# Seven quarter products in place of eight for two token blocks of the up-projections, with the blocks' order turned round

## The chip, the cores and the metric

One Trainium2 chip, one of its cores. The metric is the device time of one execution in microseconds (us); the median of several executions is compared.

## The reference, cut to what matters

One decoder layer over 1072 token columns: 32 sample tokens, 16 meta tokens and 1024 prompt tokens, model width 1024. Retention and gated DeltaNet heads are mixed first; the change lies behind them, in the output projection and the gated MLP:

```python
x = x + jnp.concatenate([o_ret, o_gdn], axis=-1) @ w_out          # 1024 x 1024
u, buf = causal_depthwise_conv(rms_norm(x, norm_ffn) @ w_up, ...) # 1024 x 5632, width 3
gate, val = jnp.split(u, 2, axis=-1)                              # 2816 each
x = x + (jax.nn.silu(gate) * val) @ w_down                        # 2816 x 1024
y = rms_norm(x, norm_final)
```

The meta tokens are dropped at the end, so the MLP works on 1058 columns (32 sample columns, 2 meta columns that the convolution needs, 1024). Outputs are float32.

## The kernel before

**Precision.** Each operand of the large projections is kept as two float32r tensors, a rounded high part and the rest: `split` casts on ScalarE and subtracts on VectorE or GpSimd. A product is three matmuls per 128 rows of the contraction: high x high, high x low, low x high (`mm3`). Tokens lie along the free dimension, features on the partitions.

**How the order is set.** Every operation is recorded with its inputs and outputs (`Recorder.add`, all instructions have line 466) and placed by a list scheduler in `flush`: per engine, the ready operation with the lowest class goes first, then the one recorded first; the costs are written into `_cost`. Buffers come from rings (`ring`, `buf`): a tile gets a slot when the planner places its first operation, in the order in which tiles were first used within their stream. The resulting order of each engine is fixed in the program. Loads are issued by SyncE (SP).

**Stages.** Up to about 630 us: input projections and head mixing. Then the part in `cp`: the last gate, and the output projection by three token blocks `BLK_B` of 384, 384 and 290 columns: `out_split` makes high and low parts of the mixed heads, `out_tile` makes one 128-row tile of one block (24 matmuls), adds the residual on VectorE, squares on ScalarE and adds the square up. Blocks 0 and 1 run together over the eight tiles of `w_out`, then block 2 with the same weights loaded again, while `norm_steps` of blocks 0 and 1 runs: sum of squares through PE, a root on VectorE (`rsqrt`), the root spread over partitions through PE, and eight normed and split tiles into `hh` and `hl`. The first gate and value tile of `w_up` are projected for blocks 0 and 1 (`early`) before block 2's norm.

**The pair loop.** For each of 22 pairs of a gate tile and a value tile: `up` loads the 1024 x 128 weights in two halves of 512 columns through `raw` into `whi`, `wlo` (two buffers each), does 24 matmuls for each of the three blocks (384, 386 and 292 columns, two of overlap for the convolution) into a bank of ring `mm` (three banks), and applies the width-3 convolution out of PSUM: one ScalarE instruction and two on VectorE. Sample columns have their own convolution with the state `su`, loaded whole at the start. Then Silu on ScalarE, gate times value on GpSimd, and a split of the result. After every second pair, `down` adds 8 tiles x 3 blocks to the residual `ob`: six matmuls into a bank of ring `mx` (five banks) and one VectorE addition each; `w_down` comes in pieces of 512 columns, split by ScalarE and GpSimd. Matmuls of projections have class 2, down sums class 1, weight splits and what empties PSUM class 0. The last two pairs end in `final`: down sums block by block, the closing norm, and the stores.

Of the kernel before, what the change touches and what calls it, by code (L numbers as in the profile page):

```python
# [45 lines left out]
BLK_B = ((0, 384), (384, 768), (768, 1058))  # L46
# [433 lines left out]
def build(tc, I, O, debug=None):  # L480
# [33 lines left out]
    ring(const, "whi", 2, KD * P, F32R)  # L514
    ring(const, "wlo", 2, KD * P, F32R)
# [48 lines left out]
    def load_w(src, lo_eng=None, tags=("raw", "raw")):  # L564
        with cls(0):
            hi = buf("whi", [P, KD, P])
            lo = buf("wlo", [P, KD, P])
            for a, tag in zip((0, 4), tags):
                raw = buf(tag, [P, 4, P])
                dma(out=raw, in_=src[:, a:a + 4, :])  # L570
                split(hi[:, a:a + 4, :], lo[:, a:a + 4, :], raw, lo_eng or V)
        return hi, lo
# [35 lines left out]
    def gate_proj(slot, nxt, tag):  # L608
# [7 lines left out]
        proj(gate_tile(slot), nxt, evac)  # L616

    with tc.tile_pool(name="mp", bufs=1) as mp:
# [78 lines left out]
        g1 = buf("whi", [P, KD, P])  # L697
        g2 = buf("wlo", [P, KD, P])
# [527 lines left out]
        keep = [v.vt for t in wq.values() for v in t]  # L1226
# [8 lines left out]
    with tc.tile_pool(name="cp", bufs=1) as cp:  # L1235
        for tag, n, e, dt in (("r15", 20, 384, F32R), ("dhl", 8, 512, F32R), ("f2k", 12, 512, F32), ("us", 1, 512, F32), ("wr", 2, 512, F32),
                              ("uo", 2, 72, F32), ("c3", 6, 4, F32)):
            ring(cp, tag, n, e, dt)
        su = cp.tile([P, 2 * NF, NB, 6], F32, name="su")
        dma(out=su, in_=I["sff"].rearrange("p (f b t) -> p f b t", f=2 * NF, b=NB))  # L1240

        def f384():
            return buf("f2k", [P, 384])

        gate_proj(3, None, "f2k")

        KS = (0, 4, 1, 5, 2, 6, 7, 3)
        wtags = (("wr", "wr"), ("raw", "raw"))
# [3 lines left out]
        def pieces(t):  # L1252
            c0, c1 = BLK_B[t]
            return ((0, NS, 0), (NS, c1, NS + 14)) if t == 0 else ((0, c1 - c0, c0 + 14),)

        def out_split(t):
            c0, c1 = BLK_B[t]
            n = c1 - c0
            if t == 0:
                o_in[t] = [[buf("r15", [P, 384]) for _ in range(KD)] for _ in range(2)]  # L1260
# [3 lines left out]
            for k in KS:  # L1264
                for a, b, s0 in pieces(t):
                    split(oh[k][:, a:b], ol[k][:, a:b], ob[:, k, s0:s0 + b - a], V if k % 2 else G)
# [5 lines left out]
            acc_of[t] = f384()  # L1272

        def out_weights(i):
            while len(wo) < min(2 * KD, i + 3):
                q = len(wo)
                wo.append(load_w(w_out[q % KD], None, wtags[q % 2]))

        def out_tile(w, m, t):
            c0, c1 = BLK_B[t]  # L1280
# [8 lines left out]
            if m == 0:  # L1289
                S.activation(acc[:, 0:n], y, AF.Square)  # L1290
            else:
                sq = f384()
                S.activation(sq[:, 0:n], y, AF.Square)
                V.tensor_tensor(out=acc[:, 0:n], in0=acc[:, 0:n], in1=sq[:, 0:n], op=ALU.add)

        def norm_block(t, acc, level=1):
            with cls(level):
                yield from norm_steps(t, acc)

        def norm_steps(t, acc):  # L1300
            c0, c1 = BLK_B[t]
            n = c1 - c0
            yield

            pss = bank()
            col, ct_, cm = (buf("c3", [P, 3]) for _ in range(3))
# [3 lines left out]
            for i, (a, b) in enumerate(cuts):  # L1310
                if b - a < P:
                    G.memset(cm, 1.0)
            ssc = buf("c3", [P, 3])
            if n % P:
                G.memset(ssc, 1.0)
                nf_ = n // P
                V.tensor_copy(ssc[:, 0:nf_], pss[:, 0:nf_])
                V.tensor_copy(ssc[0:n % P, nf_:nf_ + 1], pss[0:n % P, nf_:nf_ + 1])
            else:
                V.tensor_copy(ssc, pss[:, 0:3])  # L1320
            rsqrt(col, ssc, ct_, cm, 1.0 / D)
            yield
            rb = bank()
            dg = buf("us", [P, 3, P])
# [3 lines left out]
            for m in range(KD):  # L1328
                if m % 2 == 0:
                    yield  # L1330
                h2 = f384()
                V.scalar_tensor_tensor(out=h2[:, 0:n], in0=ob[:, m, c0:c1], scalar=nffn(m), in1=rb[:, 0:n], op0=ALU.mult, op1=ALU.mult)
                split(hh[:, m, c0:c1], hl[:, m, c0:c1], h2[:, 0:n], V if m % 2 else G)

        out_split(0)
        out_split(1)
        out_weights(0)
        for m, t in ((0, 0), (1, 0), (0, 1), (1, 1)):
            out_tile(m, m, t)
        for m in range(2, KD):  # L1340
            out_weights(m)
            for t in (0, 1):
                out_tile(m, m, t)
        out_split(2)
        others = [norm_block(0, acc_of[0]), norm_block(1, acc_of[1])]
        for m in range(KD):
            out_weights(KD + m)
            out_tile(KD + m, m, 2)
            for _ in range(5):
                next(others[m // 2 % 2], None)  # L1350
        for o in others:
            for _ in o:
                pass

        UP = ((0, 384), (382, 768), (766, 1058))

        def up(f, uo, dsts, ts=(0, 1, 2), part=None):
            hi, lo = part or load_w(w_up[f])
            i = 2 * (f // NF) + f % 2
            for t in ts:  # L1360
                b0, b1 = UP[t]
                nh = b1 - b0
                out = bank("mm")
                mm3(out[:, 0:nh], hi, lo, lambda k: hh[:, k, b0:b1], lambda k: hl[:, k, b0:b1])
                d = f384()
                dsts.append(d)
                o0, s = (NS - 2, NS) if t == 0 else (0, 0)
                n = nh - 2 - o0
                with cls(0):
                    S.activation(d[:, s:s + n], out[:, o0:o0 + n], AF.Copy, scale=cf(0, f))  # L1370
                    V.scalar_tensor_tensor(out=d[:, s:s + n], in0=out[:, o0 + 1:o0 + 1 + n], scalar=cf(1, f), in1=d[:, s:s + n],
                                           op0=ALU.mult, op1=ALU.add)
                    V.scalar_tensor_tensor(out=d[:, s:s + n], in0=out[:, o0 + 2:o0 + 2 + n], scalar=cf(2, f), in1=d[:, s:s + n],
                                           op0=ALU.mult, op1=ALU.add)
                    if t == 0:
                        S.copy(su[:, f, :, 2:6], out[:, 0:NS].rearrange("p (b t) -> p b t", b=NB))
                    if t == 2:
                        S.copy(uo[:, 64 + 2 * i:66 + 2 * i], out[:, nh - 2:nh])
                if t == 0:
                    ds_ = d[:, 0:NS].rearrange("p (b t) -> p b t", b=NB)  # L1380
                    G.tensor_scalar(out=ds_, in0=su[:, f, :, 0:4], scalar1=cf(0, f), scalar2=0.0, op0=ALU.mult, op1=ALU.add)
                    for j in (1, 2):
                        V.scalar_tensor_tensor(out=ds_, in0=su[:, f, :, j:j + 4], scalar=cf(j, f), in1=ds_, op0=ALU.mult, op1=ALU.add)
                    S.copy(uo[:, 16 * i:16 * i + 16].rearrange("p (b t) -> p b t", b=NB), su[:, f, :, 4:6])
            return hi, lo

        early = {}
        uo0 = buf("uo", [P, 72])
        for f in (0, NF):
            dst = []  # L1390
            early[f] = (up(f, uo0, dst, (0, 1)), dst)
        for _ in norm_block(2, acc_of[2], 0):
            pass


        def final(t, wd):
# [3 lines left out]
            acc = [f384(), f384()]  # L1400
            for m in range(KD):
                down(wd[m // 4], m, t, "mm")
                with cls(0):
                    sq = f384() if m > 1 else acc[m]
# [3 lines left out]
            with cls(0):  # L1408
# [8 lines left out]
                s2, rr, tt, mm = (buf("c3", [P, 3]) for _ in range(4))  # L1417
# [13 lines left out]
                dg = buf("us", [P, 3, P])  # L1431
# [9 lines left out]
        for gp in range(NF // 2):  # L1441
# [4 lines left out]
            def down_weights(mh):  # L1446
                wd = []
                for p in (2 * gp, 2 * gp + 1):
                    with cls(0):
                        raw = buf("f2k", [P, 512])  # L1450
                        dma(out=raw, in_=w_down[p * P:p * P + P, 512 * mh:512 * mh + 512])
                        dh = buf("dhl", [P, 512])
                        dl = buf("dhl", [P, 512])
                        split(dh, dl, raw, G)
                    wd.append((dh, dl))
                return wd

            for p in (2 * gp, 2 * gp + 1):
                if tail and p % 2:
                    wd = [down_weights(mh) for mh in range(2)]  # L1460
                dg, dv = ds = [], []
# [102 lines left out]
```

## Time and profile before

| | |
|---|---|
| median of 3 runs | 1553.11 us (1550.46 to 1553.45) |
| profiled execution | 1549.05 us, span 1547.2 us |
| TensorE clock, mean granted | 0.991 |
| TensorE busy | 1505.8 us (97%), 9875 matmuls |
| VectorE busy | 976.2 us (63%) |
| ScalarE busy | 582.3 us (38%) |
| GpSimd busy | 301.3 us (19%) |
| DMA | 91.06 MB, 59 GB/s |

The span runs from the first to the last instruction. PE is TensorE, PEld its weight loads, DVE VectorE, ACT ScalarE, POOL GpSimd, SP SyncE. Matmuls overlap, so the time of one is longer than the distance between two starts. A granted clock of 1.00 is 2.4 GHz.

### The profile page before, as it was taken

The numbers are of one execution on the slowest core, as the hardware profiler recorded it, in microseconds if no ns is written. First come the engines' busy times: TensorE is split into PE (matmuls) and PEld (weight loads), VectorE is DVE, ScalarE is ACT, GpSimd is POOL, SyncE is SP. The second block draws the span as 40 slices with busy tenths as digits, with TensorE's granted clock in tenths as the row PEclk, the third lists the DMA queues.
The fourth block names the chain that finished last, engine by engine and source line by source line (L and its number), as shares of the span: only waits on it lengthen the run. The fifth ranks groups of instructions, "written<-read, shape, count | busy, mean of one in ns | idle before, by whom it ended". The sixth has DMA issues, their size and how long they took to land.

```text
span 1547.2 us, 25949 instructions
## 1 busy us (share of the span) xinstructions
PE 1505.8 (97%) x9875; PEld 1453.0 (94%) x9875; DVE 976.2 (63%) x2411; ACT 582.3 (38%) x1553; POOL 301.3 (19%) x365
## 2 busy tenths in 40 slices
PE   7999999999999999999999999999999999999994
PEld 7898988999899899999999999999999999999994
DVE  4787787787768856647854545545554545555547
ACT  4553453455346335424532232324132231324123
POOL 1221202202120221501320212113020212112022
PEclk9999999999999999999999999999999999999997
DMA  5121202111120211523120110202021111202103
GB/s 189 30 72 29 84 20 70 43 59 60 41 81 28 63 33 53 183 83 96 49 76 28 56 60 25 75 23 70 20 64 28 56 52 33 68 29 70 42 1 114
DMA packets 63689, 91.06 MB, mean 59 GB/s; under 512 B 13060, under 2 KB 31948, under 8 KB 63436
## 3 DMA queue, kind: packets, MB, share of 16 engines
q1 hardware_dynamic: 63564, 89.40, 18.3%
q8 instruction: 78, 1.28, 0.4%
q14 instruction: 47, 0.39, 0.1%
HBM read 79.71 MB, written 9.66 MB: 58 GB/s over the span
## 4 chain that ended last, share of the span: by engine, by line
PE 90%; DVE 6%; DMA 1%; issue 1%; ACT 1%; POOL 0%; SPq 0%; DVEq 0%; ACTq 0%; POOLq 0%
PE mm L466 61%; PE mx L466 29%; DVE wlo L466 1%; DVE ob L466 1%; DMA ob<-in_xt 1%; DVE sw L466 1%; DVE c L466 1%; DMA gbq<-scr_rows 0%; ACT f2k L466 0%; SPq L466 0%; POOL f2k L466 0%; DVE f2k L466 0%; DVE t2k L466 0%; DVE gvb L466 0%; DVE hl L466 0%
## 5 line engine op out<-in xcount | busy, mean ns | idle before, releaser
L466 PE MATMUL mm<-hh,whi 128*128 128x384 f32 (+5 forms) x1952 | 643.5, 330 | 1.7 <-ACT hh L466 1.0
L466 PE MATMUL mm<-hh,wlo 128*128 128x384 f32 (+5 forms) x1952 | 644.5, 330 | 0.0
L466 PE MATMUL mm<-hl,whi 128*128 128x384 f32 (+5 forms) x1952 | 642.3, 329 | 0.4 <-POOL hl L466 0.3
L466 PEld LDWEIGHTS mm<-hh,whi 128*128 128x128 f32 x1952 | 368.8, 189 | 4.8 <-issue 1.5
L466 PEld LDWEIGHTS mm<-hl,whi 128*128 128x128 f32 x1952 | 369.2, 189 | 3.2 <-issue 0.9
L466 PEld LDWEIGHTS mm<-hh,wlo 128*128 128x128 f32 x1952 | 368.6, 189 | 1.7 <-issue 0.5
L466 DVE SCALAR_TENSOR_TENSOR f2k<-mm,wc,f2k 128x352 f32<-128x352 f32 (+2 forms) x264 | 150.9, 572 | 160.7 <-ACT f2k L466 80.0
L466 PE MATMUL mx<-r,dhl 128*128 128x384 f32 (+1 forms) x1440 | 232.5, 321 | 0.0
L466 PEld LDWEIGHTS mx<-r,dhl 128*128 128x128 f32 x1440 | 231.9, 188 | 0.0
L466 ACT ACTIVATE f2k<-mm,wc 128x352 f32<-128x352 f32 (+1 forms) x132 | 72.0, 545 | 306.7 <-PE mm L466 306.7
L466 DVE TENSOR_TENSOR ob<-mx,ob 128x384 f32<-128x384 f32 (+1 forms) x240 | 123.3, 524 | 100.7 <-PE mx L466 98.4
L466 DVE TENSOR_TENSOR wlo<-raw,whi 128x512 fp32r<-128x512 f32 x170 | 137.2, 820 | 33.1 <-ACT whi L466 32.6
L466 ACT CAST whi<-raw 128x512 fp32r<-128x512 f32 x170 | 103.9, 620 | 43.5 <-PE mm L466 36.0
L466 POOL TENSOR_TENSOR f2k<-f2k,f2k 128x384 f32<-128x384 f32 (+1 forms) x75 | 76.6, 1022 | 173.4 <-DVE f2k L466 160.1
L466 POOL TENSOR_SCALAR f2k<-su,wc 128x32 f32<-128x32 f32 x44 | 13.5, 306 | 443.9 <-ACT su L466 443.9
L466 POOL TENSOR_TENSOR ob<-ob,sw 128x384 f32<-128x384 f32 (+1 forms) x39 | 41.9, 1074 | 210.5 <-DVE sw L466 145.4
L466 ACT ACTIVATE f2k<-f2k 128x384 f32<-128x384 f32 (+1 forms) x66 | 32.9, 499 | 115.8 <-DVE f2k L466 115.8
L466 DVE TENSOR_TENSOR r<-f2k,r 128x384 fp32r<-128x384 f32 (+1 forms) x66 | 34.8, 528 | 60.3 <-ACT r L466 60.2
L466 ACT CAST r<-f2k 128x384 fp32r<-128x384 f32 (+1 forms) x66 | 32.4, 490 | 93.7 <-POOL f2k L466 93.7
L466 POOL TENSOR_TENSOR dhl<-f2k,dhl 128x512 fp32r<-128x512 f32 x44 | 55.6, 1298 | 11.8 <-ACT dhl L466 11.8
L466 DVE SCALAR_TENSOR_TENSOR ob<-mm,wc,ob 128x384 f32<-128x384 f32 (+3 forms) x90 | 51.3, 570 | 1.7 <-ACT ob L466 1.2
L466 DVE TENSOR_TENSOR ob<-mm,ob 128x384 f32<-128x384 f32 (+1 forms) x48 | 25.0, 522 | 38.4 <-PE mm L466 38.1
(282 smaller groups left out, 1830.7 us busy)
## 6 DMA issues: line engine op xcount, KB each, us to landing
raw<-in_w_up SPq DMA_DIRECT2D x88, 256.0 KB, 2.7
raw<-in_w_in SPq DMA_DIRECT2D x64, 256.0 KB, 2.9
f2k<-in_w_down SPq DMA_DIRECT2D x44, 256.0 KB, 4.5
raw<-in_w_out SPq DMA_DIRECT2D x18, 256.0 KB, 2.8
gbq<-scr_rows SPq DMA_DIRECT2D x16, 256.0 KB, 4.2
out<-sst SPq DMA_DIRECT2D x8, 512.0 KB, 2.6
wr<-in_w_out SPq DMA_DIRECT2D x14, 256.0 KB, 3.0
ob<-in_xt SPq DMA_DIRECT2D x4, 768.0 KB, 8.3
```

Source lines behind the costliest of these rows:

```text
L466: f(*a, **k)
```

## The change

Blocks become 510 (508 for the output projection), 274 and 274 columns. Block 0 keeps the plain product. For blocks 1 and 2, each 276 columns wide with the overlap, a pair's gate and value tiles and the two halves of the contraction form a 2 x 2 by 2 x 2 product, done with seven quarter products (Winograd's form of Strassen's) of 12 matmuls each instead of eight. The four sums of weights are made by GpSimd in the raw buffers and split like weights; the four sums of activations are made once, in the norm of blocks 1 and 2 (`norm_others`): one of them goes over block 2's first half in `hh`, `hl`, the others into new tensors `th`, `tl`. Seven VectorE additions per pair join the products out of PSUM.

The output projection does blocks 1 and 2 first, block 0 last with the weights in reverse order (the last three kept), and block 0's norm comes after pair 0's seven products are recorded, with class -1. Two banks of `mx` are set apart for the down sums (ring `dn`); `w_down` comes in quarters; weight buffers are halves (four of each, six from the MLP on; four raw ones); `su` is loaded per tile.

```diff
-BLK_B = ((0, 384), (384, 768), (768, 1058))
+BLK_O = ((0, 508), (508, 784), (784, 1058))
+BLK_B = ((0, 510), (510, 784), (784, 1058))
+WS = 276
+HB = (508, 782)
...
-    ring(const, "whi", 2, KD * P, F32R)
-    ring(const, "wlo", 2, KD * P, F32R)
+    ring(const, "whi", 4, KD * P // 2, F32R)
+    ring(const, "wlo", 4, KD * P // 2, F32R)
...
+    def unit(raw, lo_eng=None, tags=("whi", "wlo")):
+        hi, lo = (buf(t, [P, 4, P]) for t in tags)
+        split(hi, lo, raw, lo_eng or V)
+        return hi, lo
...
+        mx = R.rings["mx"]
+        R.rings["dn"] = Ring(mx.bufs)
+        mx.free.sort(key=lambda f: f[1])
+        R.rings["dn"].free = [mx.free.pop() for _ in range(2)]
+        more("raw", 2, F32)
+        more("whi", 2, F32R)
+        more("wlo", 2, F32R)
...
+        def norm_others():
+            rb1 = roots(1, acc_of[1])
+            yield
+            rb2 = roots(2, acc_of[2])
+            yield
...
+            for k in range(4):
+                b11, b12, b21, b22 = (buf("ds", [P, WS]) for _ in range(4))
+                for kk, one_, two_ in ((k, b11, b12), (4 + k, b21, b22)):
+                    normed(1, kk, rb1, one_)
+                    normed(2, kk, rb2, two_[:, 2:WS])
+                    S.copy(two_[:, 0:2], one_[:, WS - 2:WS])
+                split(hh[:, k, b1], hl[:, k, b1], b11, G)
+                split(hh[:, 4 + k, b1], hl[:, 4 + k, b1], b21, G)
+                split(hh[:, 4 + k, c0:c1], hl[:, 4 + k, c0:c1], b22[:, 2:WS], V)
+                V.tensor_tensor(out=b11, in0=b12, in1=b11, op=ALU.subtract)
+                split(hh[:, k, tcols], hl[:, k, tcols], b11, V)
+                yield
+                G.tensor_tensor(out=b12, in0=b22, in1=b12, op=ALU.subtract)
+                split(th[:, 1, k, :], tl[:, 1, k, :], b12, G)
+                V.tensor_tensor(out=b22, in0=b22, in1=b11, op=ALU.subtract)
+                split(th[:, 0, k, :], tl[:, 0, k, :], b22, V)
+                V.tensor_tensor(out=b21, in0=b21, in1=b22, op=ALU.subtract)
+                split(th[:, 2, k, :], tl[:, 2, k, :], b21, G)
+                yield
...
+        out_split(1)
+        out_split(2)
         out_split(0)
-        out_split(1)
...
+        for i in range(3):
+            out_weights(i)
+            out_tile(i, i, 1)
+        for i in range(3):
+            out_tile(i, i, 2)
+        for m in range(3, KD):
             out_weights(m)
-            for t in (0, 1):
+            for t in (1, 2):
                 out_tile(m, m, t)
+        others = norm_others()
         for m in range(KD):
             out_weights(KD + m)
-            out_tile(KD + m, m, 2)
+            out_tile(KD + m, order[KD + m], 0)
+            for _ in range(2):
+                next(others, None)
...
+        def up_pair(p, uo, late=None):
...
+                r11, r12, r21, r22 = (load_half(w_up[f], a) for f in fs for a in (0, 4))
+                a11, a12, a21, a22 = (unit(r) for r in (r11, r12, r21, r22))
+                G.tensor_tensor(out=r22, in0=r21, in1=r22, op=ALU.add)
+                G.tensor_tensor(out=r21, in0=r11, in1=r21, op=ALU.subtract)
+                G.tensor_tensor(out=r11, in0=r22, in1=r11, op=ALU.subtract)
+                G.tensor_tensor(out=r12, in0=r12, in1=r11, op=ALU.subtract)
+                s2, s1 = (unit(r) for r in (r11, r22))
+                s3, s4 = (unit(r, None, ("al", "al") if late else ("whi", "wlo")) for r in (r21, r12))
...
+            x = one(a11, B11)
+            m1 = buf("ds", [P, WS])
+            with cls(0):
+                S.copy(m1, x)
+            g1 = []
+            if late is None:
+                first_block(lambda: g1.append(second()))
+            else:
+                g1.append(second())
+            v = one(a22, T4, "mx")
+            u2 = buf("ds", [P, WS])
+            add(u2, one(s2, T2), m1)
+            z = one(s1, T1)
+            u3 = buf("ds", [P, WS])
+            add(u3, one(s3, T3), u2)
+            add(u2, z, u2)
+            v1_ = conv(add(v, v, u3), NF + p, 1, uo, None)
+            v2_ = conv(add(z, z, u3), NF + p, 2, uo, None)
+            z = one(s4, B22)
+            g2_ = conv(add(z, z, u2), p, 2, uo, None)
+            if late is not None:
+                late()
+                first_block()
...
-            def down_weights(mh):
...
+            def down_weights(mq, tags=("dhl", "dhl")):
+                with cls(0):
+                    raw = buf("rawd", [P, 2, 256])
...
-                out = bank(tag)
+                out = bank("dn")
```

`first_block` is block 0's plain product of both tiles (24 matmuls each) with its convolution; `second` is a12 x B21 joined with m1 and convolved; `one` makes a quarter product; `add` is a VectorE addition with one operand in PSUM.

## Rows read from the trace of the kernel before

**Rows 1.** The page: busy time by engine; the chain that ended last, by engine.

```profile
PE 1505.8 (97%) x9875; PEld 1453.0 (94%) x9875; DVE 976.2 (63%) x2411; ACT 582.3 (38%) x1553; POOL 301.3 (19%) x365
...
PE 90%; DVE 6%; DMA 1%; issue 1%; ACT 1%; POOL 0%; SPq 0%; DVEq 0%; ACTq 0%; POOLq 0%
```

**Rows 2.** Stretches: from:to, length, busy time by engine, PE clock, DMA share, GB/s.

```profile
710.00:740.00 30.00, 29.25 (x218) 29.05 (x217) 27.06 (x70) 13.74 (x28) 5.04 (x7) 1.00 0.34 106
740.00:770.00 30.00, 28.42 (x171) 26.72 (x171) 26.89 (x64) 17.09 (x41) 11.49 (x13) 1.00 0.12 37
...
868.60:891.70 23.10, 23.10 (x146) 23.10 (x146) 12.78 (x27) 1.96 (x5) 4.35 (x5) 1.00 0.00 1
891.70:938.50 46.80, 46.80 (x289) 46.80 (x289) 23.77 (x44) 18.05 (x43) 7.91 (x10) 1.00 0.22 69
1000.00:1200.00 200.00, 200.00 (x1240) 200.00 (x1239) 105.56 (x201) 56.09 (x135) 35.61 (x40) 1.00 0.13 41
...
1510.00:1547.20 37.20, 16.92 (x98) 15.45 (x96) 28.41 (x75) 12.81 (x31) 10.40 (x12) 0.70 0.34 118
```

**Rows 3.** The chain in order of time: start, length, what it ran through.

```profile
868.58 23.09 PE mx L466 x144
891.67 46.87 PE mm L466 x288
```

**Rows 4.** Instructions in order of time, up matmuls: start, length, line, operation, shape.

```profile
836.27 0.30 PE L466 MATMUL mm<-hh,whi 128*128 128x292 f32 x1
...
839.55 0.34 PE L466 MATMUL mm<-hh,whi 128*128 128x384 f32 x1
...
851.80 0.33 PE L466 MATMUL mm<-hh,whi 128*128 128x384 f32 x1
...
855.46 0.34 PE L466 MATMUL mm<-hh,whi 128*128 128x386 f32 x1
```

**Rows 5.** Instructions in order of time, one-column matmuls, six in each row.

```profile
38.13 0.81 PE L466 MATMUL mx<-ones_t,gvb 128*128 128x1 f32 x6
38.80 0.81 PE L466 MATMUL mx<-ones_t,gy 128*128 128x1 f32 x6
```

**Rows 6.** Instruction groups by shape, 868.6 to 938.5: busy, mean ns, idle before.

```profile
L466 DVE TENSOR_TENSOR ob<-mx,ob 128x384 f32<-128x384 f32 x16 | 8.8, 557 | 8.5 <-PE mx L466 8.4
...
L466 DVE TENSOR_TENSOR wlo<-raw,whi 128x512 fp32r<-128x512 f32 x8 | 6.9, 861 | 2.8 <-ACT whi L466 2.8
L466 POOL TENSOR_TENSOR dhl<-f2k,dhl 128x512 fp32r<-128x512 f32 x5 | 6.4, 1299 | 2.1 <-ACT dhl L466 2.1
...
L466 ACT CAST whi<-raw 128x512 fp32r<-128x512 f32 x8 | 5.0, 622 | 1.9 <-PE mm L466 1.9
L466 DVE SCALAR_TENSOR_TENSOR f2k<-mm,wc,f2k 128x384 f32<-128x384 f32 x8 | 4.9, 618 | 7.2 <-ACT f2k L466 7.1
L466 DVE SCALAR_TENSOR_TENSOR f2k<-mm,wc,f2k 128x290 f32<-128x290 f32 x8 | 4.1, 517 | 1.0 <-ACT uo L466 1.0
L466 POOL TENSOR_TENSOR f2k<-f2k,f2k 128x384 f32<-128x384 f32 x4 | 4.1, 1015 | 8.2 <-DVE f2k L466 8.2
L466 DVE TENSOR_TENSOR ob<-mx,ob 128x290 f32<-128x290 f32 x8 | 3.7, 459 | 1.5 <-PE mx L466 1.4
...
L466 DVE SCALAR_TENSOR_TENSOR f2k<-su,wc,f2k 128x32 f32<-128x32 f32 x8 | 1.9, 242 | 0.0
```

**Rows 7.** Instructions in order of time, weight subtractions with and without POOL beside them.

```profile
838.44 1.01 POOL L466 TENSOR_TENSOR f2k<-f2k,f2k 128x384 f32<-128x384 f32 x1 [3.06 <-DVE f2k L466]
838.64 1.37 DVE L466 TENSOR_TENSOR wlo<-raw,whi 128x512 fp32r<-128x512 f32 x1 [0.28 <-ACT whi L466]
...
840.86 0.69 DVE L466 TENSOR_TENSOR wlo<-raw,whi 128x512 fp32r<-128x512 f32 x1
```

**Rows 8.** Instructions in order of time, one step of a root chain.

```profile
754.61 0.16 DVE L466 TENSOR_TENSOR c<-c,c 128x3 f32<-128x3 f32 x1
```

**Rows 9.** Instructions in order of time, POOL at the tail.

```profile
1512.05 8.24 POOL L466 TENSOR_TENSOR f2k<-f2k,f2k 128x290 f32<-128x290 f32 x7 [19.18 <-DVE f2k L466]
```

More of the change, by code (lines that the diff above doesn't have):

```diff
@@ L1225, in build @@
         wq[None] = wo[0]
-        keep = [v.vt for t in wq.values() for v in t]
+        keep = [v.vt for t in wq.values() for x in t for v in x.parts]
         for v in keep:
@@ L1288, in out_tile, with roots @@
             acc = acc_of[t]
-            if m == 0:
+            if w % KD == 0:
                 S.activation(acc[:, 0:n], y, AF.Square)
             else:
-                sq = f384()
+                sq = tmp(n)
                 S.activation(sq[:, 0:n], y, AF.Square)
[L1294 to L1301, printed above, removed]
+                (G if KD < w < 2 * KD - 1 else V).tensor_tensor(out=acc[:, 0:n], in0=acc[:, 0:n], in1=sq[:, 0:n], op=ALU.add)
+        def roots(t, acc):
+            c0, c1 = BLK_O[t]
             n = c1 - c0
-            yield
             pss = bank()
-            col, ct_, cm = (buf("c3", [P, 3]) for _ in range(3))
+            col, ct_, cm = (buf("c3", [P, 4]) for _ in range(3))
             cuts = [(a, min(a + P, n)) for a in range(0, n, P)]
@@ L1338, in build, with normed, norm_first @@
-        for m, t in ((0, 0), (1, 0), (0, 1), (1, 1)):
-            out_tile(m, m, t)
-        for m in range(2, KD):
+            return rb
+        def normed(t, m, rb, h2):
+            c0, c1 = BLK_O[t]
+            V.scalar_tensor_tensor(out=h2, in0=ob[:, m, c0:c1], scalar=nffn(m), in1=rb[:, 0:c1 - c0], op0=ALU.mult, op1=ALU.mult)
+        def norm_first():
+            with cls(-1):
+                rb = roots(0, acc_of[0])
+                c0, c1 = BLK_O[0]
+                for m in range(KD):
+                    h2 = f384()[:, 0:c1 - c0]
+                    normed(0, m, rb, h2)
+                    split(hh[:, m, c0:c1], hl[:, m, c0:c1], h2, V if m % 2 else G)
@@ new lines, in prod, with cols @@
+        def prod(out, a, x, first=True, last=True):
+            with cls(2):
+                for k in range(4):
+                    xh, xl = x(k)
+                    T.matmul(out, a[0][:, k, :], xh, start=first and k == 0, stop=False)
+                    T.matmul(out, a[0][:, k, :], xl, start=False, stop=False)
+                    T.matmul(out, a[1][:, k, :], xh, start=False, stop=last and k == 3)
+        def cols(k0, sl):
+            return lambda k: (hh[:, k0 + k, sl], hl[:, k0 + k, sl])
@@ new lines, in sums, with one, add, first_block @@
+        def sums(i):
+            return lambda k: (th[:, i, k, :], tl[:, i, k, :])
+        B11, B21 = (cols(k, slice(HB[0], HB[0] + WS)) for k in (0, 4))
+        B22, T1 = cols(4, slice(HB[1], HB[1] + WS)), cols(0, slice(BLK_O[2][0], BLK_O[2][0] + WS))
+        T2, T3, T4 = (sums(i) for i in range(3))
+        def up_pair(p, uo, late=None):
+            fs = (p, NF + p)
+            sus = []
+            with cls(0):
+                for f in fs:
+                    su = buf("su", [P, NB, 6])
+                    dma(out=su, in_=I["sff"][:, f * NB * 6:(f + 1) * NB * 6].rearrange("p (b t) -> p b t", b=NB))
+                    sus.append(su)
+                r11, r12, r21, r22 = (load_half(w_up[f], a) for f in fs for a in (0, 4))
[6 more added lines that the diff above has]
+                s3, s4 = (unit(r, None, ("al", "al") if late else ("whi", "wlo")) for r in (r21, r12))
+            def one(a, b, tag="mm"):
+                out = bank(tag)[:, 0:WS]
+                prod(out, a, b)
+                return out
+            def add(out, a, b):
+                with cls(0):
+                    V.tensor_tensor(out=out, in0=a, in1=b, op=ALU.add)
+                return out
+            whole = []
+            def first_block(then=None):
+                for f, (ka, kb) in zip(fs, ((a11, a12), (a21, a22))):
+                    out = bank()[:, 0:510]
+                    prod(out, ka, cols(0, CL), last=False)
+                    prod(out, kb, cols(4, CL), first=False)
+                    whole.append(conv(out, f, 0, uo, sus[f // NF]))
+                    if then is not None and f == p:
+                        then()
+            def second():
+                x2 = one(a12, B21)
+                return conv(add(x2, x2, m1), p, 1, uo, None)
+            x = one(a11, B11)
+            m1 = buf("ds", [P, WS])
+            with cls(0):
+                S.copy(m1, x)
[18 more added lines that the diff above has]
+                first_block()
+            return (whole[0], g1[0], g2_), (whole[1], v1_, v2_)
@@ L1416, in final @@
                         prev = op
-                s2, rr, tt, mm = (buf("c3", [P, 3]) for _ in range(4))
+                s2, rr, tt, mm = (buf("c3", [P, 4]) for _ in range(4))
                 G.memset(s2, 1.0)
@@ L1444, in build @@
             tail = gp == NF // 2 - 1
[L1446 to L1468 removed]
+            def down_weights(mq, tags=("dhl", "dhl")):
+                with cls(0):
+                    raw = buf("rawd", [P, 2, 256])
+                    dma(out=raw, in_=w_down[2 * gp * P:2 * gp * P + 2 * P, 256 * mq:256 * mq + 256].rearrange("(a p) m -> p a m", a=2))
+                    dh, dl = (buf(t, [P, 2, 256]) for t in tags)
+                    split(dh, dl, raw, G)
+                return dh, dl
+            for p in (2 * gp, 2 * gp + 1):
+                dg, dv = up_pair(p, uo, norm_first if p == 0 else None)
                 row = []
```

215 lines of the change are left out of this document (106 added, 109 removed).

## The prediction

> **What bounds the kernel now.** I read the engine totals of the page first, then the chain that ended last, then the stretches, and last single instructions. TensorE (PE) is busy for 97% of the span, the next engine, VectorE (DVE), for 63%, and PE holds 90% of the chain [rows 1]. So time is lost or won on PE unless another engine takes over. The reader is to see in the stretches that the share is no average over unlike parts: from 1000 to 1200 us PE is busy for 200.00 of 200.00 us at a granted clock of 1.00, the 2.4 GHz level, with DVE at 105.56 us and GpSimd (POOL) at 35.61 us [rows 2]. That stretch is the pair loop, and it repeats: 144 down matmuls in 23.09 us, then 288 up matmuls in 46.87 us, which is two pairs [rows 3]. Nothing waits there; PE's matmuls are the price. Two stretches are different. From 710 to 770 us (second half of the out-projections, the norms, the first up-projections) PE loses 0.75 + 1.58 = 2.3 us while DVE is busy 54 of 60 us [rows 2]. In the tail, 1510 to 1547.2 us, PE works 16.92 of 37.20 us [rows 2].
>
> **The pair loop on PE.** Before, a pair has 144 up matmuls over 1062 columns in three blocks, 354 on average: 46.87 / 288 = 162.7 ns each, of which 354 / 2.4 = 147.5 ns are columns and 15.2 ns are the rest. The single starts agree: 24 matmuls of 292 columns from 836.27 to 839.55 are 136.7 ns each (15.0 beside the columns), 21 of 384 from 851.80 to 855.46 are 174.3 ns (14.3) [rows 4]. After, a pair has 48 matmuls of 510 columns and 7 x 12 = 84 of 276. By the same sum these take 212.5 + 15.2 = 227.7 ns and 115 + 15.2 = 130.2 ns: 48 x 227.7 + 84 x 130.2 = 21.87 us against 46.87 / 2 = 23.43. That is 1.57 us a pair, **34.5 us over 22 pairs**. Neither size has a row. If the slope is taken from the rows of 292 and 384 alone ((174.3 - 136.7) / 92 = 0.409 ns a column) the pair is 21.7 us and the gain 38; if only the columns shrink and the 12 missing matmuls bring nothing beside them, it is 3312 / 2.4 = 1.38 us a pair, 30. A floor under a short matmul, from its weight load, is not near: one-column matmuls with a fresh 128x128 weight start 0.67 / 6 = 112 ns apart [rows 5]. I keep 34.5, bounds 30 and 38.
>
> The Trainium skill (TensorE: Matmul & The Clock Gate, Back-to-back issue gap) has the columns plus 2.5 ns between matmuls at full clock. By it the pair would go from 144 x 150.0 = 21.6 us to 48 x 215 + 84 x 117.5 = 20.2, and the gain would be an estimate of 31 us; the rows have 14 to 15 ns beside the columns, so the missing matmuls are worth more here.
>
> The down-projections keep 1058 columns and 144 matmuls per two pairs, the out-projections 1058 columns and 576 matmuls: no term on PE.
>
> **What the pair loop adds elsewhere.** DVE first. From the rows of 384 and 290 columns [rows 6], a scalar_tensor_tensor out of PSUM is 206 ns + 1.074 a column, a tensor_tensor 157 + 1.043. Up part of one pair: convolutions 4 x 0.72 (478 columns) + 8 x 0.50 (274) = 6.9 us; the sample columns 4 x 0.243 = 1.0; the seven additions of products 7 x 0.445 = 3.1 (three of them write PSUM, which no row shows; they could be 0.3 to 0.7 each); weight subtractions 8 instead of 4, 0.69 each with no neighbour [rows 7], 5.5; activations' low parts 0.69 + 2 x 0.44 = 1.6. Together 18.1 us, where now it is 23.77 / 2 = 11.9 [rows 2]; with 6.3 for the down sums 24.4 of the new 33.4 us, 73%. But the up part alone has 18.1 of 21.9 us, 83%. On ScalarE four more casts are added, 0.62 us each [rows 6], on an engine that is busy 56 of 200 us [rows 2]: hidden, and if it weren't, 2.5 us a pair. POOL gets the four weight sums, 1.3 us each by its 512-wide row [rows 6]: 5.2 us on top of 35.61 / 200 x 35.0 = 6.2 a pair now [rows 2], a third of its time, hidden as time of POOL, though not as a neighbour of DVE.
>
> That neighbour is the cost I can't sum. A weight subtraction is 0.69 us alone, 1.37 beside a POOL tensor_tensor that started 0.2 us earlier [rows 7], and the mean of 861 ns over two pairs says that two of eight are so stretched [rows 6]. DVE has some 15 such instructions with two SBUF inputs in the up part of a pair (8 weights, 3 activations, 4 sample ones), POOL is busy for some 8.8 of the 21.9 us (5.2 and three gating products of about 1 us [rows 6], the samples' 0.6), so 15 x 0.40 x 0.68 = 4.1 us if every meeting costs a full 0.68 and 2.0 us at half: 20.1 to 22.2 us against PE's 21.9. PE can run ahead only by the banks it has (three mm, three mx, and two that the down sums now keep instead of five shared). What queues behind a late DVE is in this order: the bank that the next product wants, the next weight's low part, the down sum whose bank PE wants back. I take **0.3 us of PE waiting a pair, 6 us in all**; at the lower end it is 0 (now it is 0, with DVE at half load), at the upper end it is the first rival. SP issues 44 small state loads instead of one, two a pair, and four w_down loads per two pairs as before, now through one buffer; the DMA share there is 0.13 [rows 2], so I count nothing; each late one would show as a gap of a few us in the down sums, which the next pair's products fill.
>
> The Trainium skill (SBUF — State Buffer, SBUF: two separate sides) states that DVE with two SBUF inputs and GpSimd exclude each other for a whole instruction. By that rule a subtraction that comes right behind the start of a 1.3 us weight sum would take 2.0 us; the longest here took 1.37, behind a shorter POOL instruction. No run so far has a POOL sum of 512 beside it.
>
> **The norms and the first pair.** Blocks 1 and 2 are now projected first (8 x 2 tiles), block 0 last: 8 tiles of 24 x 226.9 ns = 43.6 us. In these 43.6 us and the 10.9 us of pair 0's seven products DVE has: 16 normed products at 0.50 = 8.0; 24 differences and low parts at 0.445 = 10.7; 8 sums at 0.69 = 5.5; 18 weight low parts = 12.4; the late norm of block 0, 8 x 0.75 + 4 x 0.69 = 8.8; additions and convolutions of the first products about 6; three root chains of about 3 us (estimate: some fifteen instructions at 0.16 to 0.2 with their gaps [rows 8]). That is 60 us against 54.5 of PE, before any meeting with POOL, which has as much to do there. A few us can be done earlier, and pair 1's first two products can fill. Now the place costs 2.3 us; I take **5 more**, bounds 0 (all of DVE's excess is hidden) and 14 (46 two-input instructions, 0.2 us each on top). Reusing three w_out weights spares 6 subtractions, which are off the path.
>
> **The rest.** Half-sized weight buffers let a load start earlier in the first 630 us, whose order is planned anew: 0, between -3 and +3. The tail: block 0 is larger and its down sums no longer wait for the last products, but POOL's run of 8.24 us over seven instructions that holds the last block's product up [rows 9] can come out either way: 0, between -6 and +5.
>
> **Sum:** -34.5 + 6 + 5 = -23.5 us. The profiled execution took 1549.05 us (span 1547.2), so 1525.5 for its like; the median shown, 1553.11, is 4 us above it, so the median after is 1553.1 - 23.5 = 1529.6: **1530 us**.
>
> **Rivals.** (1) DVE becomes the bound in the up stretches. It decides once DVE's up part plus its waits for POOL passes the old PE time, 18.1 + w > 23.4, so w > 5.3 us a pair, 0.36 for each of the 15 instructions, unless the down stretch (10.3 us free on DVE per two pairs) takes the excess. At half of a 1.3 us sum each, w = 9.8 and the pair takes 27.9 less at most 3 moved to the down stretch, 24.9: 1.5 more than now, 33 us, with the 5 of the first pair about 1590. For it: 1.37 beside 0.69, and DVE at 83% without waits. Against it: the stretched ones cost PE nothing now [rows 2].
> (2) The two down banks. A small down group takes 6 x (114.2 + 13.4) = 0.77 us on PE, its sum 0.44 on DVE; with one stretched subtraction ahead PE waits 1.37 + 0.44 - 0.77 = 1.0 us. Once a pair: 22 us, 1553.1 - 34.5 + 5 + 22 = 1546. For it: five shared banks become two; against: up matmuls stand between in the planned order.
> (3) The products do not get shorter, since a matmul has a floor near the 136.7 ns of the 292-column row: 84 x 6.5 ns = 0.55 us a pair, 12 us, 1542. The 112 ns rows speak against it.
> (4) Everything added is hidden, the first pair included: 1553.1 - 34.5 = 1519, down to 1512 with a better tail.
>
> **How the numbers follow.** The forecast, 1520 to 1545, has 0.62 (with (3), which lies in it, at 0.03); (4) 0.08; (2) and the like, 1545 to 1556, 0.16; (1) or a first pair that stands far longer, above 1556, 0.14. A difference below 0.2%, 3 us, can't be told from none here: of (2)'s 0.16 half is faster, 0.05 the same, 0.03 slower. Faster 0.78, same 0.05, slower 0.17. The range for 8 in 10 leaves out the lowest few and most of (1): 1514 to 1556.
>
> **What would show it.** Right: the chain has up stretches of 264 matmuls in about 43.7 us between down stretches of 23.1, PE near 100% there, DVE near 75%, short products starting 130 ns apart. Wrong: PE waiting for DVE or for a weight's low part inside the pair loop (1, 2), short matmuls 137 ns apart (3), or more than 15 us of idle PE between the out-projections and the second pair. Subtractions near 2 us would make (1) likely.

## The result and the profile after

The changed kernel takes 1535.82 us (median of 4 runs, 1534.65 to 1535.91) against 1552.3 us before in the same series: a ratio of 0.9893, 95% interval 0.9876 to 0.991. A second series gave 1535.52 us and 0.9909 (0.9893 to 0.9926). The forecast was 1530, within 1514 to 1556. The profiled execution took 1535.91 us (span 1534.0) where the one before took 1549.05 (1547.2): 13.1 us less, where the forecast had 23.5; by the medians it is 16.5.

The page of the changed kernel: busy time by engine, and the chain that ended last, by engine; they answer to [rows 1].

```profile
PE 1487.7 (97%) x9621; PEld 1349.4 (88%) x9621; DVE 1121.9 (73%) x2667; ACT 644.6 (42%) x1685; POOL 443.0 (29%) x487
...
PE 85%; DVE 10%; ACT 2%; issue 2%; DMA 1%; POOL 0%; SPq 0%; DVEq 0%; ACTq 0%; POOLq 0%
```

VectorE's share of the chain went from 6% to 10%: PE now waits for it somewhere. The stretches (columns as in [rows 2]; one more stretch, 700 to 740 us, has PE at 38.94 of 40.00) say where; the stretch from 630 to 800 us (end of the head mixing, out-projections, norms, first pair) is called the head below:

```profile
630.00:700.00 70.00, 64.36 (x452) 63.36 (x451) 37.73 (x67) 29.10 (x77) 23.32 (x40) 0.95 0.46 144
740.00:770.00 30.00, 22.82 (x114) 20.13 (x113) 22.15 (x38) 11.23 (x25) 17.54 (x15) 0.89 0.17 54
770.00:800.00 30.00, 27.69 (x147) 22.80 (x146) 27.70 (x52) 16.75 (x37) 16.65 (x14) 1.00 0.01 2
1000.00:1200.00 200.00, 199.69 (x1216) 180.21 (x1215) 145.63 (x274) 74.44 (x172) 69.20 (x66) 1.00 0.16 49
1500.00:1534.00 34.00, 20.68 (x146) 18.93 (x145) 26.11 (x80) 8.48 (x20) 4.77 (x8) 0.79 0.36 129
```

The pair loop is as full as before (199.69 of 200 us). Between 630 and 800 us PE idles 5.64 + 1.06 + 7.18 + 2.31 = 16.2 us, where it idled 2.3, although DVE is busy only 22 of 30 us in the worst stretch. The lower clock (0.95 and 0.89) follows the two longest waits. PE's rows of the same kernel, waits in brackets, show the four longest waits, and the pitch (the distance between two starts) of 276-column matmuls behind the wait of 5.96 us:

```profile
653.32 0.60 PE L469 MATMUL mm<-th,whi 128*128 128x276 f32 x1 [3.59 <-ACT th L469]
655.34 0.60 PE L469 MATMUL mm<-tl,whi 128*128 128x276 f32 x1 [1.43 <-DVE tl L469]
...
763.08 1.86 PE L469 MATMUL mx<-ones_t,f2k 128*128 128x1 f32 x8 [5.96 <-DVE f2k L469]
...
765.40 0.43 PE L469 MATMUL mx<-th,whix 128*128 128x276 f32 x1
...
768.85 0.38 PE L469 MATMUL mm<-th,whi 128*128 128x276 f32 x1
...
796.72 0.73 PE L469 MATMUL mx<-al,dhl 128*128 128x510 f32 x2 [2.11 <-ACT al L469]
```

From 765.40 to 768.85 there are 15 starts, 230 ns apart instead of 127: the 1.2 GHz level after a wait of 6 us. I put the clock's cost at about 2 us behind each of the two longest waits, an estimate from such starts.

The loop, as pieces of the chain (start, length): the same piece comes again after two pairs.

```profile
894.98 15.27 PE mx L469 x89
...
962.42 15.25 PE mx L469 x89
```

67.44 us here, 67.40 over the loop, against 23.09 + 46.87 = 69.96 [rows 3]: 2.55 x 11 = 28.0 us less. The account: loop -28.0; idle time from 630 to 800 us +13.9 and slow clock about +4; the out-projections start 1.4 us later, of which 0.6 is idle time already counted, so +0.8; PE idle from 1480 us to its last matmul 7.7 instead of 13.4, -5.8. Together -15.1. The other 2 us to the measured -13.1 are not traced; the out-projections' own pitches (508 columns at 229.8 ns, 276 and 274 at 127) make 0.3 of them.

### The profile page after: what moved, and what is told of

It is laid out like the page before. It is cut to its first block, busy times and chain, and to the rows that moved or that the text cites. A ratio compares the mean times of both kernels' runs of the same rounds, so it can differ in the third digit from the quotient of the medians.

```text
span 1534.0 us, 26192 instructions
## 1 busy us (share of the span) xinstructions
PE 1487.7 (97%) x9621; PEld 1349.4 (88%) x9621; DVE 1121.9 (73%) x2667; ACT 644.6 (42%) x1685; POOL 443.0 (29%) x487
## 4 chain that ended last, share of the span: by engine, by line
PE 85%; DVE 10%; ACT 2%; issue 2%; DMA 1%; POOL 0%; SPq 0%; DVEq 0%; ACTq 0%; POOLq 0%
PE mx L469 46%; PE mm L469 38%; DVE ob L469 2%; DVE wlo L469 2%; DVE ds L469 1%; DMA ob<-in_xt 1%; DVE f2k L469 1%; DVE c L469 1%; DVE sw L469 1%; DVE hl L469 1%; DVE wlox L469 0%; ACT jk L469 0%; SPq L469 0%; DVE gvb L469 0%; DVE gbq L469 0%
## 5 line engine op out<-in xcount | busy, mean ns | idle before, releaser
L469 PE MATMUL mm<-hh,whi 128*128 128x384 f32 (+5 forms) x1084 | 357.4, 330 | 1.2 <-DVE ob L469 1.2
L469 PE MATMUL mm<-hh,wlo 128*128 128x384 f32 (+5 forms) x1084 | 357.0, 329 | 0.0
L469 PE MATMUL mm<-hl,whi 128*128 128x384 f32 (+5 forms) x1084 | 356.2, 329 | 0.0
L469 PEld LDWEIGHTS mm<-hh,whi 128*128 128x128 f32 x1084 | 206.1, 190 | 7.5 <-issue 2.3
L469 PEld LDWEIGHTS mm<-hl,whi 128*128 128x128 f32 x1084 | 205.9, 190 | 5.6 <-issue 0.5
L469 PEld LDWEIGHTS mm<-hh,wlo 128*128 128x128 f32 x1084 | 206.1, 190 | 4.7 <-issue 1.3
L469 DVE TENSOR_TENSOR ob<-mx,ob 128x274 f32<-128x274 f32 (+1 forms) x264 | 136.0, 522 | 99.5 <-PE mx L469 96.4
L469 PEld LDWEIGHTS mx<-as,dhl 128*128 128x128 f32 x1008 | 143.3, 190 | 16.6 <-DVE ob L469 8.5
L469 PE MATMUL mx<-as,dhl 128*128 128x274 f32 x1008 | 153.3, 293 | 1.4 <-DVE ob L469 0.4
L469 PE MATMUL mx<-al,dhl 128*128 128x510 f32 x504 | 134.2, 395 | 3.2 <-ACT al L469 2.1
L469 DVE TENSOR_TENSOR wlo<-raw,whi 128x512 fp32r<-128x512 f32 x131 | 122.8, 939 | 11.3 <-ACT whi L469 9.1
L469 POOL TENSOR_TENSOR dhl<-rawd,dhl 128x512 fp32r<-128x512 f32 x42 | 54.5, 1297 | 132.6 <-ACT dhl L469 126.3
```

The lines of the kernel that those rows point to most:

```text
L469: f(*a, **k)
```

## The experiments

What ScalarE (ACT) did while PE stood, in two stretches of the changed kernel:

```profile
639.65 0.62 ACT L469 CAST whix<-rawx 128x512 fp32r<-128x512 f32 x1 [4.65 <-DMA rawx<-in_w_out]
640.45 0.62 ACT L469 CAST whix<-rawx 128x512 fp32r<-128x512 f32 x1 [0.19 <-DMA rawx<-in_w_out]
642.57 0.62 ACT L469 CAST dhl<-rawd 128x512 fp32r<-128x512 f32 x1 [1.49 <-DMA rawd<-in_w_down]
643.09 1.71 ACT L469 CAST th<-ob 128x276 fp32r<-128x276 f32 x5
...
652.84 0.42 ACT L469 CAST th<-ob 128x276 fp32r<-128x276 f32 x1 [0.31 <-POOL ob L469]
...
759.50 0.62 ACT L469 CAST al<-raw 128x512 fp32r<-128x512 f32 x1 [3.76 <-POOL raw L469]
760.02 0.62 ACT L469 ACTIVATE f2k<-ob 128x508 f32<-128x508 f32 x1
```

First, casts for weights stand ahead of the casts of block 1 (`th`), which the out-projection wants first; their loads go into buffers that only the new memory pool adds and are issued at 636.98, after GpSimd (POOL) has left the old pool (635.94 + 1.01). Later, the square of block 0's last row (`f2k<-ob` at 760.02, its input ready at 756.3) stands behind a cast of a summed weight that waits for POOL.

The queue behind the first stall is longer than ScalarE's: the last cast of `th`, at 652.84, waits for POOL's product for the mixed heads (`ob`), and on POOL that stands behind a subtraction for `w_down`:

```profile
649.94 1.47 POOL L469 TENSOR_TENSOR dhl<-rawd,dhl 128x512 fp32r<-128x512 f32 x1
651.37 1.44 POOL L469 TENSOR_TENSOR ob<-ob,f2k 128x384 f32<-128x384 f32 x1
```

**Theory:** these are waits in line; other orders give the time back. **Rival:** the head is short of DVE and POOL, and a wait removed comes back at the next place. A third question is what the seven products are worth by themselves.

**Block 1's split first.**

```diff
-        out_split(1)
+        with cls(-1):
+            out_split(1)
```

> The split of block 1 of the mixer output (the first operand of the out-projection) goes ahead of the other work of its engines in the planned order; nothing else is changed. Theory (the head loses to waits in line on ScalarE): the casts of the block no longer stand behind two weight casts whose loads come late, so of the 5.6 us that PE idles from 630 to 700 us at most 1.5 stay, the stretch at the lower clock behind it goes, and the time falls by 5 to 7 us, 1535.8 to about 1530. Rival (VectorE and GpSimd have too much to do there, the order on ScalarE only shows it): the subtractions come as late as before, at most 2 us are gained, 1534 to 1537.

Measured: 1529.78 us, 0.9877 (0.9859 to 0.9896). PE in the stretches 630 to 700 and 740 to 770 us:

```profile
630.00:700.00 70.00, 67.66 (x493) 66.79 (x492) 41.36 (x84) 29.44 (x78) 23.29 (x40) 1.00 0.46 144
740.00:770.00 30.00, 22.80 (x138) 21.24 (x138) 22.22 (x46) 12.81 (x25) 14.03 (x13) 0.89 0.11 36
```

2.3 us idle instead of 5.6, and the clock stays at 1.00; the second stall is untouched. The span falls from 1534.0 to 1527.0. The theory holds, though more stays than the 1.5 us expected: two waits of 0.68 and 1.66 us, for a cast and for its low part. By the ratios alone the intervals of this run and of the changed kernel overlap (0.9859 to 0.9896, 0.9876 to 0.991), and the changed kernel was not run in this series; the verdict on this run and the next rests on the rows.

**The summed casts behind the last square.**

```diff
+                aft = squares[-1:] if late else ()
-                s2, s1 = (unit(r) for r in (r11, r22))
+                s2, s1 = (unit(r, after=aft) for r in (r11, r22))
```

(and the same for s3 and s4; `unit` gives its cast these predecessors in the planned order)

> The casts of pair 0's four summed weights are held behind the last square of block 0 on ScalarE; nothing else is changed. Theory: PE's wait of 6.0 us for the block's sum of squares (757 to 763 us) falls to about 2.3, since the square is done at 757 and what is left is GpSimd's add before it (757.0 to 758.3) and VectorE's (about 0.7); with a part of the slow clock behind it 4 to 6 us, 1535.8 to about 1531. Rival (the sums are what is late, whoever waits): PE stands at the first product with a summed weight instead, at most 1 us is gained.

Measured: 1530.44 us, 0.987 (0.9857 to 0.9884). PE's wait is

```profile
759.50 0.72 PE L469 MATMUL mx<-ones_t,f2k 128*128 128x1 f32 x5 [2.97 <-DVE f2k L469]
```

2.97 us instead of 5.96, with the granted clock of the stretch at 0.94 instead of 0.89. As the theory had it, 0.7 us short.

**Both, with work moved from POOL to DVE.**

```diff
-                (G if KD < w < 2 * KD - 1 else V).tensor_tensor(out=acc[:, 0:n], ...
+                (G if KD < w < 2 * KD - 2 else V).tensor_tensor(out=acc[:, 0:n], ...
-                    G.tensor_tensor(out=dg[t][:, 0:n], ...
+                    (V if p < 2 and t != 1 else G).tensor_tensor(out=dg[t][:, 0:n], ...
```

> Both edits together, the add of the square before last moved from GpSimd to VectorE, and the gating products of blocks 0 and 2 of the first two pairs on VectorE instead of GpSimd (these stood behind the weight sums when the first down sum wanted them, 2.25 us). Theory: the gains add, 10 to 14 us, about 1523 (1519 to 1527), and PE's idle time from 630 to 800 us is under 6 us instead of 16. Rival: 1532 or more, the idle time only moves.

Measured: 1527.62 us, 0.9857 (0.9841 to 0.9873), beside the range, with 11.3 us idle instead of under 6. By the rows the two moves did harm, though no run has the two edits by themselves. An addition moved to DVE met POOL, and the down sum that was to gain waited longer than in the run above (0.76):

```profile
749.36 1.74 DVE L469 TENSOR_TENSOR f2k<-f2k,f2k 128x508 f32<-128x508 f32 x1 [0.17 <-ACT f2k L469]
...
754.17 1.05 PE L469 MATMUL mx<-ones_t,f2k 128*128 128x1 f32 x8 [3.55 <-DVE f2k L469]
787.16 0.73 PE L469 MATMUL mx<-al,dhl 128*128 128x510 f32 x2 [3.05 <-ACT al L469]
```

**Eight products instead of seven.** Each quarter pair accumulates in PSUM; the sums of weights, columns and products are gone, the rest stays.

```diff
+            def whole_of(f, t, ka, kb, xa, xb, tag="mm"):
+                out = bank(tag)[:, 0:WS]
+                prod(out, ka, xa, last=False)
+                prod(out, kb, xb, first=False)
+                return conv(out, f, t, uo, None)
```

> The seven-product form alone is undone: eight quarter products accumulate in PSUM, there are no sums of weights, of columns or of products; block sizes, the order of the out-projection, the late norm, the half-sized weight buffers and the two down banks stay. Theory (PE bounds the loop and the products themselves are the gain): 24 more matmuls of 127.3 ns per two pairs, the period goes from 67.40 to 70.45 us, 33.6 us over 22 pairs; the head gives back some 8 us, as the sums that held it up are gone: 1561 (1553 to 1570), slower than before the change. Rival (part of the gain is the regrouping into blocks and banks, or the sums cost something in the loop): a period under 69.9, 1550 or less.

Measured: 1553.82 us, 1.0018 (1.0009 to 1.0027). The recurring piece of its chain:

```profile
837.18 8.53 PE mx L469 x48
...
906.92 8.54 PE mx L469 x48
```

69.74 us for two pairs, 69.75 over the loop. Head: 8.2 us idle instead of 16.2, the 8 that I had put there. The time is inside the theory's range, at its lower end. So the regrouping alone gives the loop 0.2 us per two pairs and the whole time nothing; the gain is the seven products'. But they bring 2.34 us per two pairs, where 24 matmuls of 127.3 ns are 3.05. The rival's mark for the period (under 69.9) was met, by its second half: the sums cost the loop 0.7. Its mark for the time (1550 or less) was not.

**The weight sums on DVE.** The four sums of a pair, all as this one:

```diff
-                G.tensor_tensor(out=r22, in0=r21, in1=r22, op=ALU.add)
+                V.tensor_tensor(out=r22, in0=r21, in1=r22, op=ALU.add)
```

> The four sums of weights of a pair on VectorE instead of GpSimd; nothing else. VectorE gets 4 x 0.69 us a pair, 145.6 + 16.6 of 200 us in the loop, 81%, GpSimd loses its 5.2 us a pair and with it most of its meetings with VectorE. Theory (PE bounds the loop with room on VectorE): the period of two pairs stays at 67.4 +- 0.2 us, the time within 3 us of the changed kernel. Rival (VectorE's queue is near the point where PE waits for it, as the 0.27 us at the down sums hint): the period rises by 0.5 us or more, over 5 us in all. A period that falls (by up to 0.5 us) would show that the meetings with GpSimd cost more than the work.

Beside it the changed kernel once more:

> The changed kernel as it is, beside the others of this series on one chip, so that gains of a few us are read against it and not only against the kernel before. 0.9893 of the time before.

Measured: 1527.55 us, 0.9856 (0.9842 to 0.9871), the changed kernel 1535.52 us. Its loop stretch and recurring piece:

```profile
1000.00:1200.00 200.00, 200.00 (x1224) 181.81 (x1223) 151.45 (x300) 75.61 (x174) 38.68 (x42) 1.00 0.17 50
```
```profile
893.05 22.50 PE mx L469 x138
959.90 22.56 PE mx L469 x138
```

66.8 us for two pairs, 0.6 less: the third outcome. DVE does more work (151.45 instead of 145.63 us) and PE waits less. In 200 us 16.6 us of sums were added, so 10.8 us of stretching went away (subtractions of weights from 45.2 to 38.6 us, additions for the sample columns from 9.0 to 5.8). PE's waits at the down sums (about 40 ns on average at each turn from an up matmul to a 274-column down sum, 0.4 us per two pairs, and some 0.2 more inside the down sums) are gone. These gaps are too short to show as idle time, since a matmul's row lasts 0.29 us while the next starts 0.13 us later: the windows told of 0.1 us, the starts of 0.6.

**PE's pitch by itself.** Behind the end of the changed kernel, groups of 12 matmuls with a fresh weight each:

```diff
+                    ops = [T.matmul(out, hh[:, (i + k) % KD, 128 * (k % 4):128 * (k % 4) + 128], hl[:, (i + k + 3) % KD, 0:n], ...
```

> The changed kernel with a stretch added behind its end, whose results go nowhere: matmuls in groups of 12, each with a fresh 128x128 weight, of 510, 384, 292, 276 and 128 columns with no other engine at work, then of 510 and 276 with VectorE additions beside. Theory (the pitch is TensorE's own): 510 columns start 230 to 231 ns apart, 276 127 ns, as in the pair loop, with additions beside or not; 128 columns not below 107 to 112 ns. Rival (the long ones are stretched by other engines' traffic): 224 to 228 ns alone and 231 with VectorE beside.

VectorE's additions came earlier than planned, beside the first stretch. Rows: 510 columns with DVE at work (busy 26.00 of 26 us), 276 columns alone, 510 alone:

```profile
1540.84 26.34 PE L469 MATMUL mx<-hl,hh 128*128 128x510 f32 x115
```
```profile
1612.76 11.52 PE L469 MATMUL mx<-hl,hh 128*128 128x276 f32 x90
```
```profile
1635.81 21.33 PE L469 MATMUL mx<-hl,hh 128*128 128x510 f32 x93
```

Less the last one's own duration (0.39 and 0.29 us): 25.95 / 114 = 227.6 ns, 11.23 / 89 = 126.2, 20.94 / 92 = 227.6. 128 columns came 111.1 ns apart. The theory holds for 276 and 128 columns and fails for 510, which go at 230.2 ns in the loop's up products and 231.6 in its down sums: that is not PE's own. The rival's cause fails too, as DVE beside it changes nothing. What does (ScalarE's or GpSimd's work, transfers, waits on results, the operands, which differ too) stays open; it is 96 x 2.6 + 48 x 4.0 ns, 0.44 us per two pairs. Nor is the bare pitch always the shorter one: 384 columns came 175.5 ns apart there and 174.6 in the loop of the kernel before.

**Orders that hold up.** The two single edits, and the sum of squares taken later by PE:

```diff
-                late()
+                late(done[2:3])    # done[2]: last matmul of the third product
```

> The two single edits that worked (block 1's split first, the casts of pair 0's summed weights behind the last square), and PE takes block 0's sum of squares after the third product of pair 0 instead of after its first matmul. The two moves of work from GpSimd to VectorE are left out: they came out 1.74 us an addition beside GpSimd, and one down sum waited 3.05 us instead of 0.76. Theory (waits in line, each of its own): the gains of the two add, and 1.5 us of the 2.97 us that PE still waits for the sum of squares are filled by the product: 7 to 11 us less than the changed kernel, 0.983 to 0.986 of the time before. Rival (the head is short of VectorE and GpSimd, and what is gained at one wait is lost at the next): no better than the better of the two edits, 0.987.

Measured: 1526.04 us, 0.9845 (0.9829 to 0.9861), 9.5 us less than the changed kernel beside it. PE's waits from 750 to 758 us are now smaller and three:

```profile
753.74 1.05 PE L469 MATMUL mx<-ones_t,f2k 128*128 128x1 f32 x8 [1.60 <-DVE f2k L469]
755.51 0.40 PE L469 MATMUL mm<-th,whi 128*128 128x276 f32 x1 [0.73 <-ACT whi L469]
757.09 0.60 PE L469 MATMUL mm<-th,wlo 128*128 128x276 f32 x1 [1.06 <-DVE wlo L469]
```

So the rival is not all wrong: a part of that wait comes back at the next summed weight. The two single edits had come to 5 to 6 us each, in another series, so the later sum of squares shows no gain of its own. From 630 to 800 us 9.3 us of idle time are left, and what it would take to remove them stays open.

**And the sums on DVE**, beside these three edits, in all pairs or in all but the first:

```diff
-                G.tensor_tensor(out=r22, in0=r21, in1=r22, op=ALU.add)
+                (G if late else V).tensor_tensor(out=r22, in0=r21, in1=r22, op=ALU.add)    # the second; late: pair 0
```

> The last head version (block 1's split first, summed casts behind the last square, sum of squares after the third product) and all weight sums on VectorE. Theory (the two gains have different places: 9.5 us in the head, 0.6 us per two pairs in the loop): 16 us less than the changed kernel, about 1519, 0.980 of the time before (0.978 to 0.982). Rival (the head is short of VectorE, so sums on it take back what the order gave): 0.984.

> As the other of this pair, but pair 0 keeps its sums on GpSimd and only pairs 1 to 21 have them on VectorE. Theory: the same loop, and pair 0's sums beside VectorE's work instead of in it, 0 to 2 us less than with all sums on VectorE. Rival (in the head too a meeting with GpSimd costs VectorE more than the sums themselves): 1 to 3 us more.

Measured: 1518.87 us, 0.9785 (0.9771 to 0.9798), and 1519.70 us, 0.9787 (0.9773 to 0.98). The gains of head and loop add; for pair 0 the engine makes no difference that these runs can tell. The first is faster than both kernels, by 33 and some 17 us (the changed kernel by its time in the series above).

## Why the prediction came out as it did

The direction and the main term were right, the time lay in the range, and the sum was too hopeful by 7 to 10 us, because **one step was mis-sized: "The norms and the first pair"**. "I take **5 more**, bounds 0 ... and 14" measured about 18 (13.9 idle, about 4 of clock), outside its own bounds. The tail, put at nothing, hid a part of that by coming out 5.8 us shorter, which was luck. I added up DVE's work (60 us) against PE's (54.5) and asked how much overflows. That overflow was not all of the cost, and the order was a large part of it: ScalarE, which had no part in that sum, held the items that PE needed behind items that waited for a transfer or for POOL, and PE, in order too, stood before a small matmul with other products ready. Three reorderings, with no work removed, gave 9.5 of the 18 back. With the sums gone altogether, in the run with eight products, the second stall is gone too (no idle time from 740 to 800 us), so the rest may be work or order; the runs don't part the two. A lower clock as the price of a stall was no term at all.

**Pair loop on PE: right in sum, by errors that cancel.** Forecast -34.5 + 6, measured -28.0. The 276-column matmul takes 127.3 ns (forecast 130.2), the 510-column one 230.2 (227.7, its bare pitch to 0.1 ns). Up: 96 x 230.2 + 168 x 127.3 = 43.5 us per two pairs against 46.87, a gain of 37 in all, between the bounds of 30 and 38. "No term on PE" for the down sums was wrong by 0.48 us per two pairs (48 x 231.4 + 96 x 129.8 = 23.57 against 23.09 [rows 3]), 5 us in all, part of it the waits. On the Trainium skill's issue gap (TensorE: Matmul & The Clock Gate, Back-to-back issue gap), 2.5 ns beside the columns, which the page gives for an isolated matmul: bare rows have 227.6 - 212.5 = 15.1 and 126.2 - 115 = 11.2 here, so the rows were the better guide.

**"0.3 us of PE waiting a pair, 6 us in all": right.** 0.6 per two pairs by the starts, 0.6 x 11 = 6.6 us, and the run with the sums on DVE got them back. The larger part of it stood where the second rival had it, a down sum's result behind a stretched subtraction, at 0.3 of its price of 22 us. Once in two pairs the chain of the changed kernel has

```profile
892.92 0.26 DVE ob L469
893.18 0.10 issue
893.28 1.28 DVE wlo L469
894.57 0.37 DVE ob L469
894.98 15.27 PE mx L469 x89
```

with PE's next start 0.26 us late and the one behind it another 0.10; the other 0.2 us per two pairs stand behind VectorE instructions that nothing stretched. What stretched this one was not a sum of weights but the low part of `w_down`, which GpSimd makes in both kernels:

```profile
892.73 1.29 POOL L469 TENSOR_TENSOR dhl<-rawd,dhl 128x512 fp32r<-128x512 f32 x1 [4.07 <-ACT dhl L469]
```

With the sums on VectorE the order came out so that the subtraction in that place takes 0.68 us. So at this place the time came back by another order of the queues; that moving such sums would always do it is not shown.

**The cost that I couldn't sum, DVE beside POOL.** POOL's sums took 1.28 us, DVE's additions out of PSUM 446 ns (forecast 0.445), DVE's busy share was 145.63 / 200 = 73%, as forecast. The worst meetings cost more than "a full 0.68". The two rows of one in the changed kernel:

```profile
884.12 1.79 DVE L469 TENSOR_TENSOR wlox<-raw,whix 128x512 fp32r<-128x512 f32 x1
```
```profile
884.06 1.29 POOL L469 TENSOR_TENSOR rawx<-rawx,raw 128x512 f32<-128x512 f32 x1
```

DVE's 0.69 us become 1.79, and it ends 0.56 us after POOL does. The Trainium skill (SBUF — State Buffer, SBUF: two separate sides) says that the one that starts second is blocked for the whole instruction of the other; this row agrees, within 0.13 us. The mean was as priced: of 128 weight subtractions from 895 to 1435 us 48 were stretched, to 1.41 us, and 80 took 0.69, so three of a pair's eight cost 0.72 us each. With the four additions for the sample columns (373 ns instead of 243) that is 2.7 us a pair, inside the 2.0 to 4.1 of the forecast and far from the 9.8 of the first rival.

**The rest.** "0, between -3 and +3" for the first 630 us: +1.4 by the start of the out-projections, and "no term" for these: +0.3. Tail "0, between -6 and +5": -5.8. I followed neither up.

**Rivals.** (1) fell: no up stretch waits for DVE, even at 76% busy with the sums on it. (2) see above. (3) fell: 127.3 ns, and the bare 128-column pitch of 111.1 puts the floor beside the 112 ns of [rows 5]. (4), "everything added is hidden", 1519, is what the kernel reached with three orders changed and the sums on VectorE (1518.87), though not by hiding everything: some 9 us of idle time are left from 630 to 800 us, and the tail's 5.8 us help. That the two numbers agree is chance.

**Signs.** DVE near 75% and PE near 100% in the loop came. Up stretches of 264 matmuls between down stretches did not: the planned order mixes the two (an up matmul starts at 894.49 between groups of down matmuls). In place of 43.7 + 23.1 = 66.8 us for two pairs there are 67.40, the 0.6 us of waits more.

## What to carry to other kernels

Where a stage joins several engines, adding up each one's work does not price it: list for each in-order queue what stands ahead of the item that the bound engine wants next, and what that one waits for. A long stall on TensorE can be paid a second time in clock: here about 2 us each behind waits of 3.6 and 6.0 us. In this loop a two-input addition was cheaper on VectorE, busy for 73%, than on GpSimd, busy for 35%: it took 0.69 us instead of 1.28, and VectorE's other work lost 10.8 us of stretching in 200 us. In the head the same kind of move brought a VectorE addition of 1.74 us beside GpSimd, so look at what runs beside it.

## What was not expected of the hardware

Short waits hide in rows of overlapping matmuls (0.6 us per two pairs by the starts, 0.1 by busy time). A 510-column matmul goes at 227.6 ns alone and beside VectorE additions, and at 230 to 232 in the loop, for a reason that stays open.
